# A token tile's latent norms and transposes stand behind the next tile's products, with a second pair of PSUM banks, and the first output row is written ahead of the last head's end

## The chip, the core and the metric

The kernel runs on one core of one Trainium2 chip. The metric is the device time of the whole kernel in microseconds (us). One core has a matrix engine (PE, with its weight loads listed apart as PEld), a vector engine (DVE), a scalar engine (ACT), a general engine (POOL) and DMA queues, of which SP's is the main one. Each engine takes its own instructions strictly in the order in which they stand, and waits on semaphores for the others.

## What is computed

A decoder trunk of two layers on 1024 tokens of width 1024. The second layer's mixer is a multi-head latent attention, and the change lies in it:

```python
def mla_mixer(h, cos, sin, w_in, q_norm_g, kv_norm_g, w_uq, w_ukv, w_out):
    proj = h @ w_in                                   # 1024 -> 384 + 256 + 64
    c_q, c_kv, k_rope = proj[..., :384], proj[..., 384:640], proj[..., 640:]
    q = (rmsnorm(c_q, q_norm_g) @ w_uq).reshape(B, T, 8, 128 + 64)
    kv = (rmsnorm(c_kv, kv_norm_g) @ w_ukv).reshape(B, T, 8, 128 + 128)
    ...
    q_rope = apply_rope(q_rope, cos[:, :, None, :], sin[:, :, None, :])
    k_rope = apply_rope(k_rope, cos, sin)
    o = causal_mla_attention(q_nope, q_rope, k_nope, k_rope, v)
    return o.reshape(B, T, 8 * 128) @ w_out
```

Around it stand a gated DeltaNet layer, two gated feed-forward blocks and the adaLN modulation, none of which the change touches.

## The kernel before

Every product is made three times over, on operands split in a high and a low part (`mm3`: high with high, high with low, low with high).

**The latent stage** is `mla_in`. The 1024 tokens are eight tiles of 128, taken in the order 0, 2, 4, 6, 1, 3, 5, 7; I call them step 0 to step 7. For a tile, `norm` loads the row, normalizes it, transposes it in eight 128x128 blocks (tile `nrm_p`), applies shift and scale on ACT (`nrm_h`) and splits it (`whi`, `wlo`); `norm` of a tile stands one tile ahead. Then come the **products** of the tile: 24 matmuls with 384 columns into one bank (`pq`, the query latent) and 24 with 320 columns into another (`pk`, the key latent and the key's rope part; both tiles have the name `pq` in the trace). Then come what I call the tile's **latents**, in seven pieces:

1. The query latent is squared and summed on ACT (L211), its 1/rms is made by a small DVE and a small POOL instruction (L213, L219), ACT scales it into the tile `mx` (L1189), and PE transposes it in three blocks ("x3", L1192).
2. The same for the key latent, with two transposes ("x2"). `mx` has one buffer, so that the key's square (which uses `mx` as scratch) waits until PE has read the query's `mx` for x3.
3. DVE multiplies each transposed latent by its gain (`mhx`), and both are split into `cq` and `ckv`.
4. The key's rope part is turned by DVE (L1112 to L1114), copied by ACT (L1115), and transposed by PE ("krt", one block, L1200).
5. Nine matmuls make the rope part of the query for all heads from `cq` ("wqr", 512 columns, tile `pr`).
6. DVE turns it (six instructions), ACT copies it (`rt`, L1115), and PE transposes it in eight blocks ("rt", L1211).
7. ACT and DVE split that into `qr`, and SP stores it.

Six PSUM tiles of a tile's latents come from the pool `pd`, which has four banks; `pq` has two, and `nrm_p` two. After the eight tiles, `mla_kq` makes head 0's keys and queries in two halves of 512 tokens (the first needs tiles 0 to 3, which are the steps 0, 4, 1 and 5, the second the steps 2, 6, 3 and 7), and `mla_v` the values of the first two heads (both into `nrm_p`).

**The attention** (`mla_attn`) goes through eight heads with four query blocks each; scores, softmax and the product with the values of different blocks are kept apart by a list `late`. Behind the last head stands the output projection, eight rows of 128 tokens (`out_row`: it loads the heads' outputs and the residual row, splits, multiplies with the first four heads' weights into two `pd` banks and adds).

What stands in the source is not quite what the engines get: the framework places instructions by priority and readiness in a time of its own, and may put a later piece of source ahead of an earlier one that isn't ready. The order that comes out is fixed when the program is built.

Of the kernel before, what the change touches and what calls it, by code (L numbers as in the profile page):

```python
# [9 lines left out]
F32 = mybir.dt.float32  # L10
# [9 lines left out]
P = 128  # L20
T = 1024
D = 1024
NT = T // P
KT = D // P
# [5 lines left out]
QR, KVR, RP = 384, 256, 64  # L30


class Trunk:
# [1099 lines left out]
    def mla_in(self):  # L1133

        nc, tc, a, v = self.nc, self.tc, self.a, self.nc.vector
        self.hq = [self.mla_st.enter_context(tc.tile_pool(name="hq", bufs=1))]
        self.hv = [self.mla_st.enter_context(tc.tile_pool(name="hv", bufs=1))]
        mp = self.mp = self.mla_st.enter_context(tc.tile_pool(name="mp", bufs=1))
        self.cq = [mp.tile([P, 3, T], F32R, name=f"cq{i}") for i in range(2)]
        self.ckv = [mp.tile([P, 2, T], F32R, name=f"ckv{i}") for i in range(2)]  # L1140
        self.kr = [mp.tile([P, T], F32R, name=f"kr{i}") for i in range(2)]
        self.qr_dram = self.dram.tile([P, H, T], F32, name="qr_dram")
        gqs = self.const.tile([P, 3], F32, name="gqs")
        v.tensor_scalar(out=gqs, in0=self.gq, scalar1=float((128 + 64) ** -0.5), op0=ALU.mult, scalar2=None)
        with ExitStack() as st:
            pool = st.enter_context(tc.tile_pool(name="mn", bufs=2))
            ps = st.enter_context(tc.tile_pool(name="mnp", bufs=2, space=PSUM))
            shift = self.mod[1, 0]
            A = self.norm_coef(self.gmix[1], self.mod[1, 1], "Am1")
            w = self.mw  # L1150
            src = a["mla_w_uq"][0].rearrange("(r p) (h n) -> p r h n", p=P, n=192)[:, :, :, 128:192]
            wqr = [self.load_w(src[:, r], shape=(H, 64), pool=pool, bufs=1, tag=f"wqr{r}_") for r in range(3)]

            def norm(t):
                x = self.mwp.tile([P, D], F32, name="xin", bufs=1)
                nc.sync.dma_start(out=x, in_=self.x_dram[t])
                y = self.mwp.tile([P, D], F32, name="nrm_x")
                r = self.rstd_of(x, self.mwp, junk=y)
                v.tensor_scalar(out=y, in0=x, scalar1=r, op0=ALU.mult, scalar2=None)
                hi = self.wsp.tile([P, KT, P], F32R, name="whi")  # L1160
                lo = self.wsp.tile([P, KT, P], F32R, name="wlo")
                for k0 in range(0, KT, 4):
                    pt = ps.tile([P, 4, P], F32, name="nrm_p")
                    h = self.mwp.tile([P, 4, P], F32, name="nrm_h")
                    for k in range(4):
                        kt = k0 + k
                        nc.tensor.transpose(pt[:, k], y[:, kt * P:(kt + 1) * P], self.ident)
                    for k in range(4):
                        kt = k0 + k
                        nc.scalar.activation(out=h[:, k], in_=pt[:, k], func=AF.Identity, scale=A[:, kt:kt + 1],  # L1170
                                             bias=shift[:, kt:kt + 1])
                    self.split(h, hi[:, k0:k0 + 4], lo[:, k0:k0 + 4])
                return hi, lo
            order = (0, 2, 4, 6, 1, 3, 5, 7)
            ahead = norm(order[0])
            for i, t in enumerate(order):
                hi, lo = ahead
                if i + 1 < NT:
                    ahead = norm(order[i + 1])
                lt = [(hi[:, kt], lo[:, kt]) for kt in range(KT)]  # L1180
                pq = ps.tile([P, QR], F32, name="pq")
                self.mm3(pq, lt, [(w[kt][0][:, 0:QR], w[kt][1][:, 0:QR]) for kt in range(KT)])
                pk = ps.tile([P, KVR + RP], F32, name="pq")
                self.mm3(pk, lt, [(w[kt][0][:, QR:], w[kt][1][:, QR:]) for kt in range(KT)])
                ts = slice(t * P, (t + 1) * P)
                for src, n, g, dst in ((pq, QR, gqs, self.cq), (pk[:, 0:KVR], KVR, self.gkv, self.ckv)):
                    y = pool.tile([P, n], F32, name="mx", bufs=1)
                    r = self.rstd_of(src, pool, n, junk=y)
                    nc.scalar.activation(out=y, in_=src, func=AF.Copy, scale=r)  # L1189
                    pt = self.pd.tile([P, n // P, P], F32, name="pd")  # L1190
                    for j in range(n // P):
                        nc.tensor.transpose(pt[:, j], y[:, j * P:(j + 1) * P], self.ident)  # L1192
                    h = pool.tile([P, n // P, P], F32, name="mhx", bufs=1)
                    v.tensor_tensor(out=h, in0=pt, in1=g.rearrange("p (a o) -> p a o", o=1).broadcast_to(
                        [P, n // P, P]), op=ALU.mult)
                    self.split(h, dst[0][:, :, ts], dst[1][:, :, ts])
                kr = pool.tile([P, 1, 2, 64], F32, name="krt")
                self.rope(kr, pk[:, KVR:].rearrange("p (a b) -> p a b", a=1), t, pool, 1)
                pt = self.pd.tile([P, P], F32, name="pd")
                nc.tensor.transpose(pt, kr.rearrange("p a b c -> p (a b c)"), self.ident)  # L1200
                self.split_ps(pt, self.kr[0][:, ts], self.kr[1][:, ts])

                pr = self.pd.tile([P, H, 64], F32, name="pd")
                self.mm3(pr, [(self.cq[0][:, r, ts], self.cq[1][:, r, ts]) for r in range(3)], wqr)
                rt = pool.tile([P, H, 2, 64], F32, name="rt", bufs=1)
                self.rope(rt, pr, t, pool, H)
                qr = pool.tile([P, H, P], F32R, name="qr", bufs=1)
                for h0 in (0, 4):
                    pt = self.pd.tile([P, 4, P], F32, name="pd")
                    for i in range(4):  # L1210
                        nc.tensor.transpose(pt[:, i], rt[:, h0 + i].rearrange("p b c -> p (b c)"), self.ident)  # L1211
                    qh = qr[:, h0:h0 + 4]
                    nc.scalar.copy(qh, pt)
                    v.tensor_tensor(out=qh[64:128], in0=pt[64:128], in1=qh[64:128].bitcast(F32), op=ALU.subtract)
                nc.sync.dma_start(out=self.qr_dram[:, :, ts], in_=qr.bitcast(F32))

            A, B, C = [self.mwp.tile([P, D], F32, name=n, **kw).bitcast(F32R)
                       for n, kw in (("nrm_x", {}), ("nrm_x", {}), ("xin", {"bufs": 1}))]
            r2, r3, r22 = [lambda y: y.rearrange("p (r n) -> p r n", n=P)] * 2 + [
                lambda y: y.rearrange("p (r h n) -> p r h n", r=2, n=P)]  # L1220
            self.kq, self.V = {}, {}
            for g in (self.mla_kq(0, ps, self.kq, ((r2(A[:, 0:256]), r2(A[:, 256:512])),
                                                        (r3(A[:, 512:896]), r3(B[:, 512:896]))), "nrm_p", 2),
                      self.mla_v(0, ps, self.V, (r22(B[:, 0:512]), r22(C[:, 0:512])), "nrm_p", 2)):
                for _ in g:
                    pass
# [117 lines left out]
    def mla_attn(self, right):  # L1344

        nc, tc, a = self.nc, self.tc, self.a
        with ExitStack() as st:
# [4 lines left out]
            early = ExitStack()  # L1352
# [11 lines left out]
            kq, V, late = self.kq, self.V, []  # L1364
            for h in range(H):
# [13 lines left out]
                    late.append((h, qq, pes, V[h // 2], wk, pb))  # L1379
                for _ in steps:  # L1380
                    pass
            self.mla_pv(*late[0])
            self.mla_pv(*self.mla_pt(*late[1]))
            early.close()

            self.out_pools(1, right)
            w_out = a["mla_w_out"][0]
            gate = self.gate_row(1, 2, self.wraw, "wraw", None)
            ws = self.out_w((0, 1), w_out, gate)
# [5 lines left out]
                self.split(raw, w[:, 0], w[:, 1])  # L1395
                ws.append((w[:, 0], w[:, 1]))
            self.bank = lambda: self.pd.tile([P, 512], F32, name="pd")
            for t in range(NT):
                x = self.mp.tile([P, 3, T], F32R, name=f"cq{t % 2}")[:, 0].bitcast(F32)
                o = self.mp.tile([P, 2, T], F32R, name=f"ckv{t % 2}")[:, :, 0:512].rearrange("p i (h t) -> p i h t", h=4)  # L1400
                self.out_row(t, 0, ws, self.x_dram[t], x, self.wraw.tile([P, 4, P], F32, name="wraw"), o[:, 0], o[:, 1],
                             self.bank)
                nc.sync.dma_start(out=self.x_dram[t], in_=x)
                if t == 2:
                    self.ow = self.out_w((4, 5), w_out, gate, self.own)
            self.ow += self.out_w((6, 7), w_out, gate)
# [101 lines left out]
```

## Time and profile before

| | before |
|---|---|
| device time, median of 3 runs | 2616.04 us (2610.63 to 2622.59) |
| the profiled execution: device time | 2613.28 us |
| its span, first to last instruction | 2611.6 us |
| PE busy | 2505.5 us, 96% of the span |
| DVE busy | 1962.5 us, 75% |
| ACT busy | 1173.5 us, 45% |
| mean granted PE clock | 0.988 of full |

The latent stage lies about from 1461 to 1586 us of the span, and the passage from the attention to the output rows about from 1815 to 1850. A row of a timeline gives the start, the duration, the engine, the line, the operation, the tiles (out<-in) and the count; in brackets behind it stands the idle time of the engine just before, and what ended it. Matmuls overlap: one begins before the one ahead of it ends, so the distance of two starts, not the duration, is what a matmul costs in a run of them.

### The profile page before, as it was taken

How to read it: one execution, taken by the hardware profiler on the slowest of the kernel's cores; microseconds unless marked ns; L12 is line 12 of the kernel's file. 1: busy time of each engine (PE TensorE's matmuls, PEld its weight loads, DVE VectorE, ACT ScalarE, POOL GpSimd, SP SyncE). 2: the span in 40 equal slices, each digit the busy share in tenths (PEclk: the TensorE clock that was granted, in tenths of full speed). 3: DMA queues.
4: the chain of work that ended last, by engine and by line, in shares of the span. 5: the costliest groups of instructions: out<-in, count | busy, mean ns of one | idle time of the engine just before them, and what ended most of it. 6: DMA issues, size and time to landing. Idle time of an engine off the chain costs nothing.

```text
span 2611.6 us, 35555 instructions
## 1 busy us (share of the span) xinstructions
PE 2505.5 (96%) x12757; PEld 2058.1 (79%) x12757; DVE 1962.5 (75%) x3748; ACT 1173.5 (45%) x2374; POOL 171.5 (7%) x322
## 2 busy tenths in 40 slices
PE   6999999999999999999999899999999999999998
PEld 5777777777778888888888798888779888887886
DVE  5787789888758888877586766668577777774778
ACT  5555454555465222322344665555283332332343
POOL 1211111221000000000000010000010000000000
PEclk8999999999999999999999999999999999999999
DMA  6111222331454544544945521112643332336634
GB/s 228 41 33 33 75 79 85 89 102 62 153 181 142 182 153 155 160 147 156 314 146 153 155 70 60 47 51 87 216 157 96 108 108 93 108 104 224 226 94 145
DMA packets 258705, 327.62 MB, mean 125 GB/s; under 512 B 17578, under 2 KB 176448, under 8 KB 258528
## 3 DMA queue, kind: packets, MB, share of 16 engines
q1 hardware_dynamic: 235840, 284.37, 34.7%
q10 hardware_dynamic: 22688, 40.97, 4.2%
q8 instruction: 101, 1.65, 0.3%
q14 instruction: 76, 0.62, 0.1%
HBM read 247.16 MB, written 78.14 MB: 125 GB/s over the span
## 4 chain that ended last, share of the span: by engine, by line
PE 77%; DVE 11%; ACT 4%; DMA 3%; issue 2%; POOL 2%; ACTq 0%; POOLq 0%; DVEq 0%; SPq 0%
PE pd L971 14%; PE nrm_p L202 14%; PE pj L202 14%; PE pd L202 10%; PE P L202 8%; PE pd L1288 3%; PE po L202 2%; DVE cacc L334 2%; PE pq L202 1%; PE tp L1331 1%; DVE X L423 1%; DVE st L421 1%; ACT Xs L441 1%; DVE wlo L178 1%; PE d L511 1%
## 5 line engine op out<-in xcount | busy, mean ns | idle before, releaser
L971 PE MATMUL pd<-wlo,gh 128*128 128x512 f32 x616 | 243.9, 396 | 2.5 <-DVE wlo L178 2.0
L971 PE MATMUL pd<-whi,gl 128*128 128x512 f32 x616 | 241.3, 393 | 0.9 <-DVE gl L178 0.9
L971 PE MATMUL pd<-whi,gh 128*128 128x512 f32 x616 | 236.9, 394 | 3.7 <-ACT gh L177 3.3
L202 PE MATMUL pj<-hThi,whi 128*128 128x512 f32 x480 | 197.0, 410 | 0.0
L202 PE MATMUL pj<-hThi,wlo 128*128 128x512 f32 x480 | 196.5, 409 | 0.0
L202 PE MATMUL pj<-hTlo,whi 128*128 128x512 f32 x480 | 196.0, 408 | 0.0
L177 ACT CAST gh<-wraw 128x1024 fp32r<-128x1024 f32 x84 | 82.3, 979 | 247.4 <-PE pd L971 209.2
L177 ACT CAST whi<-wraw 128x1024 fp32r<-128x1024 f32 (+3 forms) x105 | 100.8, 961 | 143.8 <-DMA wraw<-in_ffn_w_gate_dram 54.2
L178 DVE TENSOR_TENSOR gl<-wraw,gh 128x1024 fp32r<-128x1024 f32 x84 | 95.2, 1133 | 63.9 <-ACT gh L177 63.4
L971 PEld LDWEIGHTS pd<-wlo,gh 128*128 128x128 f32 x616 | 116.3, 189 | 33.3 <-DVE wlo L178 8.1
L219 POOL TENSOR_TENSOR nrm_r<-nrm_r,mh 128x1 f32<-128x1 f32 x56 | 37.4, 669 | 1585.3 <-DVE nrm_r L213 965.7
L971 PEld LDWEIGHTS pd<-whi,gh 128*128 128x128 f32 x616 | 116.2, 189 | 30.4 <-ACT gh L177 4.2
L178 DVE TENSOR_TENSOR wlo<-wraw,whi 128x1024 fp32r<-128x1024 f32 (+3 forms) x105 | 117.5, 1119 | 28.6 <-ACT whi L177 26.4
L971 PEld LDWEIGHTS pd<-whi,gl 128*128 128x128 f32 x616 | 116.3, 189 | 26.6 <-DVE gl L178 1.5
L202 PE MATMUL nrm_p<-T,xrow 128*128 128x512 f32 (+1 forms) x576 | 133.7, 387 | 0.0
L202 PE MATMUL nrm_p<-T,ow_hi 128*128 128x512 f32 (+1 forms) x600 | 132.0, 369 | 0.0
L202 PE MATMUL nrm_p<-T,ow_lo 128*128 128x512 f32 (+1 forms) x552 | 125.8, 376 | 0.0
L202 PEld LDWEIGHTS nrm_p<-T,xrow 128*128 128x128 f32 x576 | 105.3, 189 | 23.5
L202 PEld LDWEIGHTS nrm_p<-T,ow_hi 128*128 128x128 f32 x600 | 103.8, 189 | 20.6 <-ACT fh L791 0.2
L202 PEld LDWEIGHTS nrm_p<-T,ow_lo 128*128 128x128 f32 x552 | 98.0, 189 | 20.4
L334 DVE SCALAR_TENSOR_TENSOR cacc<-cr,cwc,cacc 128x512 f32<-128x512 f32 x144 | 108.5, 760 | 3.3 <-ACT cacc L332 2.8
L202 PEld LDWEIGHTS pj<-hTlo,whi 128*128 128x128 f32 x480 | 92.0, 192 | 15.4
(531 smaller groups left out, 6399.0 us busy)
## 6 DMA issues: line engine op xcount, KB each, us to landing
wraw<-in_ada_w_dram SPq DMA_DIRECT2D x80, 512.0 KB, 4.1
wraw<-in_ffn_w_gate_dram SPq DMA_DIRECT2D x44, 512.0 KB, 3.9
wraw<-in_ffn_w_up_dram SPq DMA_DIRECT2D x44, 512.0 KB, 4.4
gd_S<-sx ACTq DMA_DIRECT2D x88, 256.0 KB, 2.5
B<-in_ffn_w_down_dram SPq DMA_DIRECT2D x40, 512.0 KB, 6.8
wraw<-gd_S SPq DMA_DIRECT2D x40, 512.0 KB, 5.1
gd_A<-co ACTq DMA_DIRECT2D x66, 256.0 KB, 2.1
wraw<-in_gdn_w_in_dram SPq DMA_DIRECT2D x32, 512.0 KB, 4.6
```

The source lines that it names most:

```text
L177: nc.scalar.copy(hi, raw)
L178: nc.vector.tensor_tensor(out=lo, in0=raw, in1=hi.bitcast(F32), op=ALU.subtract)
L202: nc.tensor.matmul(out, l, r, start=(i == 0), stop=(i == len(seq) - 1))
L219: self.nc.gpsimd.tensor_tensor(out=out, in0=in_, in1=self.mh[:, 0:in_.shape[1]], op=ALU.pow)
L334: nc.vector.scalar_tensor_tensor(out=acc, in0=cr[:, j:j + 512], scalar=self.cw[:, j, ch:ch + 1], in1=acc, op0=ALU.mult, op1=ALU.add)
L421: v.tensor_tensor(out=t[:, 0:n], in0=Lr[:, j, j + 1:32].rearrange("p (i o) -> p i o", o=1).broadcast_to([P, n, 8]), in1=X[:, j:j + 1].broa ...
L423: v.tensor_tensor(out=X[:, j + 1:32], in0=X[:, j + 1:32], in1=t[:, 0:n], op=ALU.subtract)
L441: nc.scalar.copy(Xs[pb, :, b * 32:b * 32 + 32].rearrange("p m (r c) -> p m r c", c=8), Xn[pb, :, :, mh].rearrange("p c r m -> p m r c"))
L511: nc.tensor.matmul(psn, kd, y, start=True, stop=True)
L971: nc.tensor.matmul(acc[t], x[:, j, ts], y[:, j], start=(j0 + j == 0 and k == 0), stop=(j0 + j == NJ - 1 and k == 2))
L1288: nc.tensor.matmul(sc[:, 0:nm], q[:, ts], k[:, cs], start=(i == 0), stop=(i == 4 and not last))
L1331: nc.tensor.transpose(pt[:, kt - k0], pes[qi][:, kt * P:(kt + 1) * P], self.ident)
```

## The change

In `mla_in` the body behind the products becomes a function `latents(t, pq, pk)`, and the loop calls it one tile late: tile t's latents are written behind the products of the tile after it. So two tiles' products are alive at once. Those of the steps 0, 2, 4, 6 go to the two banks of `pq` as before, those of the steps 1, 3, 5, 7 to two of the four banks of `pd`, which the latents use as well. In `mla_attn` the output weights' preparation and output row 0 move ahead of the last query block's end.

```diff
+            def latents(t, pq, pk):
+
                 ts = slice(t * P, (t + 1) * P)
...
+            order = (0, 2, 4, 6, 1, 3, 5, 7)
+            ahead, last = norm(order[0]), None
+            for i, t in enumerate(order):
+                hi, lo = ahead
+                if i + 1 < NT:
+                    ahead = norm(order[i + 1])
+                lt = [(hi[:, kt], lo[:, kt]) for kt in range(KT)]
+                b, nm = ((ps, "pq"), (self.pd, "pd"))[i % 2]
+                pq = b.tile([P, QR], F32, name=nm)
+                self.mm3(pq, lt, [(w[kt][0][:, 0:QR], w[kt][1][:, 0:QR]) for kt in range(KT)])
+                pk = b.tile([P, KVR + RP], F32, name=nm)
+                self.mm3(pk, lt, [(w[kt][0][:, QR:], w[kt][1][:, QR:]) for kt in range(KT)])
+                if last:
+                    latents(*last)
+                last = t, pq, pk
+            latents(*last)
...
-            self.mla_pv(*late[0])
-            self.mla_pv(*self.mla_pt(*late[1]))
-            early.close()
-
-            self.out_pools(1, right)
...
-            for t in range(NT):
+
+            def row(t):
...
+            self.mla_pv(*late[0])
+            row(0)
+            self.mla_pv(*self.mla_pt(*late[1]))
+            early.close()
+            self.out_pools(1, right)
+            for t in range(1, NT):
+                row(t)
```

The next rows are those of PE, of before, at a tile in the middle of the latent stage: from one tile's rt to the next tile's krt. Matmuls into `pq` are the products of the next tile.

```order
L1211 MATMUL pd<-ident,rt 128x128 x8
L202 MATMUL pq<-wmi_hi,whi 128x320
...
L1192 MATMUL pd<-ident,mx 128x128 x3
L1167 MATMUL nrm_p<-ident,nrm_x 128x128 x8
L202 MATMUL pq<-wmi_hi,whi 128x384
...
L1192 MATMUL pd<-ident,mx 128x128 x2
L202 MATMUL pq<-wmi_hi,whi 128x384
...
L1200 MATMUL pd<-ident,krt 128x128
```

And these are PE's of the change, from step 2's rt through step 3's latents to step 5's products (line numbers moved: x3 and x2 are L1183, krt L1191, rt L1202).

```order
L1202 MATMUL pd<-ident,rt 128x128 x8
L1183 MATMUL pd<-ident,mx 128x128 x3
L1167 MATMUL nrm_p<-ident,nrm_x 128x128 x5
L1183 MATMUL pd<-ident,mx 128x128 x2
L1191 MATMUL pd<-ident,krt 128x128
L202 MATMUL pd<-wqr_hi,cq_13670 128x512
...
L202 MATMUL pq<-wmi_hi,whi 128x384
...
L1202 MATMUL pd<-ident,rt 128x128 x8
L202 MATMUL pd<-wmi_hi,whi 128x384
```

Nine products and eight transposes stood between x3 and x2, now five transposes; fifteen products stood between x2 and krt, now nothing. The products of step 5 (into `pd`) come only behind step 3's last transposes.

At the end of the stage, PE of before, from the last tile's products to its last transposes; matmuls into `nrm_p` are `mla_kq`'s.

```order
L202 MATMUL pq<-wmi_hi,wlo 128x320
L1192 MATMUL pd<-ident,mx 128x128 x3
L202 MATMUL nrm_p<-ckv_13672,nrm_x 128x512
...
L1192 MATMUL pd<-ident,mx 128x128 x2
L202 MATMUL nrm_p<-cq_13670,nrm_x 128x512
...
L1200 MATMUL pd<-ident,krt 128x128
L202 MATMUL pd<-wqr_hi,cq_13670 128x512
...
L202 MATMUL nrm_p<-ckv_13672,nrm_x 128x512
...
L1211 MATMUL pd<-ident,rt 128x128 x8
```

And PE of the change at the same place, from step 7's products through step 6's and into step 7's latents.

```order
L202 MATMUL pd<-wmi_hi,wlo 128x320
L1183 MATMUL pd<-ident,mx 128x128 x5
L1191 MATMUL pd<-ident,krt 128x128
L202 MATMUL pd<-wqr_hi,cq_13670 128x512
...
L1202 MATMUL pd<-ident,rt 128x128 x8
L1183 MATMUL pd<-ident,mx 128x128 x5
L202 MATMUL nrm_p<-ckv_13672,nrm_x 128x512
L202 MATMUL nrm_p<-cq_13670,nrm_x 128x512
L1191 MATMUL pd<-ident,krt 128x128
```

Two tiles' latents now stand behind the last products, step 6's with no other work of PE between its pieces. The whole order of the change on PE, as what stands between a tile's pieces ("384" and "320" are products with so many columns, "norm" 128x128 transposes of a later tile's `norm`, "kq" matmuls of `mla_kq`; the pieces of one tile never stand between another's):

| step | x3 to x2 | x2 to krt | wqr to rt |
|---|---|---|---|
| 0 | 8 norm, 5 of 384 | 11 of 384 | 8 of 384, 12 of 320 |
| 1 | 8 norm | 4 norm | 4 norm, 18 of 384 |
| 2 | 6 of 384, 8 norm | 5 of 320 | 19 of 320, 3 norm |
| 3 | 5 norm | nothing | 18 of 384 |
| 4 | 6 of 384 | 6 of 320 | 18 of 320 |
| 5 | nothing | 2 kq | 13 kq |
| 6 | nothing | nothing | nothing |
| 7 | nothing | 2 kq | 13 kq |

At the end of the attention, PE of before, behind the last but one query block's products (`tp` are transposes of the softmax, `po` the products with the values, matmuls into `pd` the output rows'):

```order
L1331 MATMUL tp<-ident,pe 128x128 x7
L202 MATMUL pd<-whi,ckv_18416 128x512
L202 MATMUL pd<-V_18406,ckv_18416 128x512 x3
...
L1331 MATMUL tp<-ident,pe 128x128 x4
L202 MATMUL pd<-V_18412,ckv_18416 128x512
...
L202 MATMUL po<-PT_18320,V_17042 128x256
L202 MATMUL pd<-V_18412,ckv_18416 128x512
L202 MATMUL pd<-whi,ckv_18452 128x512
```

And the change there:

```order
L202 MATMUL pd<-whi,ckv_18349 128x512
L202 MATMUL pd<-V_18317,ckv_18349 128x512 x3
L202 MATMUL pd<-V_18323,ckv_18349 128x512 x3
L1338 MATMUL tp<-ident,pe 128x128 x7
L202 MATMUL pd<-whi,ckv_18452 128x512
...
L1338 MATMUL tp<-ident,pe 128x128 x8
L202 MATMUL pd<-V_18317,ckv_18452 128x512
L202 MATMUL po<-PT_18384,V_17042 128x256
```

Output rows' matmuls stood among the last head's in both; a few more stand ahead of the last transposes now. On SP's queue one store of the last head's output moves behind three loads, and nothing else changes there.

## Rows read from the trace of the kernel before

**Rows 1.** Windows: from:to, length, busy us of PE PEld DVE ACT POOL, PEclk, DMA.

```profile
1475.20:1575.90 100.70, 96.22 (x590) 88.26 (x591) 66.47 (x199) 68.26 (x178) 11.86 (x22) 1.00 0.24 73
1815.00:1850.00 35.00, 34.19 (x213) 28.99 (x212) 25.99 (x54) 18.01 (x46) 1.55 (x6) 1.00 0.34 110
```

**Rows 2.** Waits of PE, 1475.2 to 1575.9: total us, times, longest.

```profile
PE pd L1192 <- ACT mx L1189: 3.9, 5, 2.5
```

**Rows 3.** Timeline of step 0, all engines, from x3 to x2.

```profile
1477.70 0.55 PE L1192 MATMUL pd<-ident,mx 128*128 128x128 f32 x3 [2.53 <-ACT mx L1189]
...
1478.35 0.38 ACT L211 ACTIVATE mx<-pq 128x256 f32<-128x256 f32 x1
...
1478.85 0.15 DVE L213 TENSOR_SCALAR nrm_r<-nrm_ss 128x1 f32<-128x1 f32 x1
...
1479.09 0.55 POOL L219 TENSOR_TENSOR nrm_r<-nrm_r,mh 128x1 f32<-128x1 f32 x1 [2.05 <-DVE nrm_r L213]
...
1479.67 0.48 ACT L1189 ACTIVATE mx<-pq,nrm_r 128x256 f32<-128x256 f32 x1
...
1480.20 0.44 PE L1192 MATMUL pd<-ident,mx 128*128 128x128 f32 x2
```

**Rows 4.** Timeline of step 6, from x2 to the copy for krt.

```profile
1555.52 0.44 PE L1192 MATMUL pd<-ident,mx 128*128 128x128 f32 x2 [0.43 <-ACT mx L1189]
...
1556.65 0.19 DVE L1114 TENSOR_TENSOR krt<-rp,rp 128x32 f32<-128x32 f32 x1
...
1556.88 0.25 ACT L1115 COPY krt<-krt 128x64 f32<-128x64 f32 x1
```

**Rows 5.** Timeline of step 7, from wqr's last matmul to rt.

```profile
1571.84 0.39 PE L202 MATMUL pd<-wqr_hi,cq 128*128 128x512 f32 x1
...
1572.26 0.42 DVE L1112 TENSOR_TENSOR rp<-pd,cos 128x256 f32<-128x256 f32 x1 [1.47 <-PE pd L202]
...
1574.38 0.62 ACT L1115 COPY rt<-rt 128x512 f32<-128x512 f32 x1 [0.85 <-DVE rt L1114]
...
1575.06 1.09 PE L1211 MATMUL pd<-ident,rt 128*128 128x128 f32 x8
```

**Rows 6.** Timeline, step 0's copy for krt, and x3 and x2 of step 1.

```profile
1482.40 0.26 ACT L1115 COPY krt<-krt 128x64 f32<-128x64 f32 x1
...
1489.21 0.49 PE L1192 MATMUL pd<-ident,mx 128*128 128x128 f32 x3
...
1492.43 0.44 PE L1192 MATMUL pd<-ident,mx 128*128 128x128 f32 x2 [0.30 <-ACT mx L1189]
```

**Rows 7.** Timeline of PE in unbroken runs, for the distance of starts.

```profile
1474.14 1.03 PE L1167 MATMUL nrm_p<-ident,nrm_x 128*128 128x128 f32 x8
...
1479.13 0.34 PE L202 MATMUL pq<-wmi_hi,whi 128*128 128x384 f32 x1
...
1480.00 0.34 PE L202 MATMUL pq<-wmi_hi,wlo 128*128 128x384 f32 x1
...
1485.10 0.31 PE L202 MATMUL pq<-wmi_hi,wlo 128*128 128x320 f32 x1
...
1487.89 0.31 PE L202 MATMUL pq<-wmi_hi,whi 128*128 128x320 f32 x1
...
1572.75 2.22 PE L202 MATMUL nrm_p<-cq,nrm_x 128*128 128x512 f32 x9
```

**Rows 8.** Timeline of PE, one wait in the feed-forward stage.

```profile
1946.83 0.39 PE L202 MATMUL P<-B,wlo 128*128 128x256 f32 x1 [2.79 <-DVE nrm_r L213]
```

**Rows 9.** Windows of 2 us behind that wait, columns as in rows 1.

```profile
1946.00:1948.00 2.00, 1.17 (x9) 1.18 (x10) 2.00 (x5) 1.85 (x4) 1.84 (x2) 0.94 0.57 229
1948.00:1950.00 2.00, 2.00 (x11) 1.90 (x11) 1.90 (x5) 2.00 (x4) 0.00 (x0) 0.50 0.02 6
1950.00:1952.00 2.00, 2.00 (x15) 2.00 (x15) 2.00 (x4) 1.16 (x3) 0.00 (x0) 0.71 0.61 180
```

More of the change, by code (lines that the diff above doesn't have):

```diff
@@ L1173, in norm @@
                 return hi, lo
[L1174 to L1184, printed above, removed]
+            def latents(t, pq, pk):
                 ts = slice(t * P, (t + 1) * P)
```

## The prediction

> **What bounds the kernel now.** I read the page first: PE is busy in 96% of the span, and PE carries most of the chain that ended last. A change gains here what PE idles, and loses what it makes PE wait. So I read the windows of the two stretches that the change touches. In the latent stage, from the end of step 0's products to the first `mla_v` matmul, PE is busy in 96.22 of 100.70 us, so it idles 4.48 us. In the passage to the output rows it idles 0.81 of 35 us [rows 1]. All other work of PE is the same matmuls as before. More than 5.3 us can therefore not be won by filling PE, and that is 0.2% of the time. PE's waits put 3.9 of the 4.48 us on the scaled latent that x3 and x2 transpose [rows 2], and 2.53 of it on one place, step 0's x3 [rows 3].
>
> What a measurement of this kernel can tell from no change I take as 0.5%, 13 us.
>
> **What a tile's latents ask of PE.** Between x3 and x2, x2 and krt, and wqr and rt, a tile's latents leave PE for ACT, DVE and POOL and come back, and something else has to stand on PE there. From the timelines I take two prices for each place: bare, where little else stood on ACT and DVE, and loaded, where the next tile's `norm` stood among them.
>
> (a) x3 to x2: the key's square waits for x3 to leave `mx`, then come the sum, DVE, POOL, the scale. At step 0, x2 starts 2.50 us behind x3's start; less x3's own 0.55, PE needs cover for 1.95 us, bare [rows 3]. At step 1 it starts 3.22 us behind, and PE idled 0.30 us, so that this was a true end of a wait; less 0.49, that is 2.73 us loaded [rows 6].
>
> (b) x2 to krt: at step 6 x2 ended at 1555.96 and ACT's copy at 1557.13, with DVE's six small instructions between: 1.2 us bare [rows 4]. At step 0 x2 ended at 1480.64 and the copy at 1482.66: 2.0 us loaded [rows 3, 6].
>
> (c) wqr to rt: 1572.23 to 1575.06, 2.83 us [rows 5]. ACT did little else there, so I use it as both.
>
> Cover on PE, by the distance of starts [rows 7]: a product with 384 columns 0.174 us (five in 0.87), with 320 columns 0.147 (nineteen in 2.79), eight `norm` transposes 1.03, a `kq` matmul 0.23 (nine in 2.22, the last 0.39 of it). Before, nine products and eight transposes covered (a) with 2.6 us, fifteen products (b) with 2.6, and 21 products (c) with 3.1; hence the few tenths of idle time in the middle of the stage.
>
> **What the change removes.** Step 0's x3 no longer stands ahead of step 1's products: 48 products, 7.7 us, go first, and its 2.53 us go. I give the change the whole 4.48 us.
>
> **What it adds.** The products of the steps 1, 3, 5, 7 need two `pd` banks, from the same pool of four that the latents go through. So in the order that comes out, the products of step 3 stand behind all of step 1's latents, step 5's behind step 3's, step 7's behind step 5's. Products then come in pairs and latents in pairs, and the odd steps' latents find little left to cover them. At the end step 6's and step 7's latents both stand behind the last products, and the first half of `mla_kq`, which covered the last tile before, has been used up at step 5. Cover from the table of the change, against the needs; what is missing in us, bare and loaded:
>
> - step 0: cover 1.90, 1.91, 3.15: 0.05 and 0.9
> - step 1: 1.03, 0.5, 3.6: 1.6 and 3.2
> - step 2: 2.07, 0.74, 3.2: 0.5 and 1.9
> - step 3: 0.65, 0, 3.1: 2.5 and 4.1
> - step 4: 1.04, 0.88, 2.65: 1.4 and 3.0
> - step 5: 0, 0.46, 3.0: 2.7 and 4.3
> - step 6: 0, 0, 0: 6.0 and 7.6
> - step 7: 0, 0.46, 3.0: 2.7 and 4.3
>
> The sums are 17.4 and 29.3 us. At the steps 0 to 4 `norm` of later tiles still stands among ACT's instructions (five scale-and-shift instructions ahead of step 3's key latent), so I take loaded there: 13.1. At the steps 5 to 7 ACT has nothing of `norm` left, so bare: 11.4. Together 24.5 us of new idle time.
>
> **The clock.** A wait of 2.79 us for DVE [rows 8] was followed by windows of 2 us at 0.94, 0.50 and 0.71 of full clock, so near its lower level of 1.2 GHz [rows 9]; less full clock that is 0.12 + 1.00 + 0.58, 1.7 us lost. The wait of 2.53 us at step 0 was followed by none, since the stage's mean is 1.00 [rows 3, 1]. The new waits at the steps 3 and 5 to 7 are 1.2 to 2.9 us, several in a row with little work between. I count one to two such dips, 2 us; the bounds are 0 and 6.
>
> [...]
>
> **The output row.** Output rows' matmuls stood among the last head's before as well; the order was already so. A few more now stand ahead of the last transposes, which can only take from the 0.81 us that PE idled there [rows 1]: I count 0.3 us won, between 0.8 won and 0.3 lost. On SP one store moves behind three loads; the heads that it holds are read only in the second half of the projection, eight rows later, so it waits for nobody. Pools opened later cost nothing.
>
> **Sum.** 24.5 - 4.5 + 2 - 0.3 = 21.7 us. The profiled execution took 2613.28 us, so 2635 us. That execution lies 2.8 us under the median of 2616.04; I set the forecast on the execution.
>
> **Rivals.**
>
> *Bare waits only.* If each handoff takes its bare price, since ACT and DVE, with PE slower, have emptied their queues, and no dip comes: 17.4 - 4.5 - 0.3 = +12.6, 2626 us, within 0.5%. For it speaks that ACT is busy in only 68 of 100.7 us and DVE in 66 [rows 1]. Against it: they take instructions in order, and `norm` of a later tile stands ahead of the piece that PE waits for.
>
> *Everything runs ahead (the other side).* While PE does 7.7 us of another tile's products, ACT and DVE could finish a tile's query and key latents, so that x3 and x2 need no cover; this decides if the key's square can start before PE's x3. Then nothing of (a) and (b) is left, only step 6's (c): 2.8 - 4.5 - 0.3 = -2, 2611 us, not slower. Against it: `mx` has one buffer, so that the key's chain starts behind x3 in each tile, and the rows of step 0 show just that sequence [rows 3].
>
> *Cold clock through the end.* From step 5's x3 to the first `mla_v` matmul stand some 11 us of waits in about 30 us. If PE fell to half its clock over the 19 us of work in there for as much as half of it, that is 9 us more in place of 2, and with loaded prices at the steps 5 to 7 (4.8 more) +33: 2647 us. The Trainium skill has such a case ("TensorE: Matmul & The Clock Gate", "A second HAM failure mode: psum-queue depth-cycling"): small idle times between groups of matmuls that go around the banks make the clock swing. For it here: a fall at 2.79 us [rows 8, 9]. Against it: none at 2.53 us.
>
> **Chances and range.** The forecast (waits about as summed, 2629 to 2642) 0.66; bare waits only 0.15; everything ahead 0.04; cold clock 0.15. Faster by over 0.5% would need 13 us, more than twice what PE idles in both stretches: 0.02, left for what I have not seen. Within 0.5% fall the bare case, the case on the other side but for that, and a small part of the forecast's low end: 0.18. Slower: 0.80. The range runs from 2621, below the bare case by a few us for handoffs that are covered after all, to 2647, the cold case.
>
> **What will show it.** In the profile after: PE's idle time in the latent stage of some 24 us in place of 4.5, ended by ACT at x3/x2 and krt, and by ACT's copy at rt of step 6; the first `mla_v` matmul at about 1597 in place of 1576; the wait of 2.53 us gone; PE clock under 1.00 in a window behind step 5; the passage to the output rows as before. I am wrong if PE idles under 12 us there, or if the second products of a pair stand in time beside the odd steps' latents; and if the stage is as said and the end still isn't, then something downstream gave it back.

## The result and the profile after

The change makes the kernel slower: 2649.64 us, median of 4 runs (2645.94 to 2653.91), against 2619.32 us, median of 4 runs of before (2610.63 to 2623.91). The ratio is 1.011, 95% interval 1.0088 to 1.0132. The forecast was 2635 us, with a range of 2621 to 2647: the direction was right, and the time lies 2.6 us above the range. The profiled execution of the change took 2650.61 us, 37.3 us more than that of before.

Windows of the change, from the end of the `norm` transposes behind step 0's products to the first `mla_v` matmul, and the passage to the output rows (columns as in rows 1):

```profile
1475.20:1610.76 135.56, 110.86 (x593) 97.15 (x591) 68.19 (x200) 69.10 (x178) 13.39 (x22) 0.87 0.18 54
1849.86:1884.86 35.00, 34.20 (x213) 28.98 (x212) 27.30 (x56) 18.46 (x46) 1.55 (x6) 1.00 0.39 128
```

They answer to [rows 1]. The passage is as it was: PE idles 0.80 us of 35, as against 0.81. The latent stage has become 34.9 us longer, and two things are to be read in its row. PE idles 135.56 - 110.86 = 24.70 us in place of 4.48, so 20.2 more. And PE is *busy* 14.6 us longer, with the same matmuls, at a granted clock of 0.87 in place of 1.00.

Waits of PE in that stretch (line waited at, releaser: total us, times, longest), against [rows 2] (L1180 is ACT's scale into `mx`, which was L1189; `rp` is the tile that DVE's turn writes):

```profile
PE pd L1183 <- ACT mx L1180: 14.2, 8, 3.2
PE pd L1191 <- ACT krt L1115: 3.2, 3, 1.5
PE pd L1202 <- ACT rt L1115: 3.0, 2, 2.8
PE nrm_p L202 <- ACT ckv L177: 2.0, 2, 1.0
PE pq L202 <- DVE rp L1112: 1.6, 2, 0.8
PE nrm_p L1167 <- ACT nrm_h L1170: 0.6, 1, 0.6
```

The wait of 2.53 us at step 0's x3 [rows 3] is gone; x2 now waits in all eight tiles.

Timeline of the change at step 3, PE and what it waits for:

```profile
1527.35 0.49 PE L1183 MATMUL pd<-ident,mx 128*128 128x128 f32 x3
1527.67 0.71 PE L1167 MATMUL nrm_p<-ident,nrm_x 128*128 128x128 f32 x5
...
1528.25 0.40 ACT L211 ACTIVATE mx<-pd 128x256 f32<-128x256 f32 x1
...
1528.62 1.86 ACT L1170 ACTIVATE nrm_h<-nrm_p,col,Am 128x128 f32<-128x128 f32 x5
...
1531.09 0.47 ACT L1180 ACTIVATE mx<-pd,nrm_r 128x256 f32<-128x256 f32 x1 [0.20 <-POOL nrm_r L219]
...
1531.61 0.69 PE L1183 MATMUL pd<-ident,mx 128*128 128x128 f32 x2 [3.23 <-ACT mx L1180]
...
1533.82 0.48 PE L1191 MATMUL pd<-ident,krt 128*128 128x128 f32 x1 [1.52 <-ACT krt L1115]
...
1534.52 0.63 PE L202 MATMUL pd<-wqr_lo,cq 128*128 128x512 f32 x1
...
1535.80 0.63 PE L202 MATMUL pd<-wqr_lo,cq 128*128 128x512 f32 x1
```

This is place (a) with the mechanism that was forecast, at more than its loaded price: x2 starts 4.26 us behind x3, and less x3's own 0.49 us that is 3.77 us, against 2.73. The square follows x3 in `mx`, five scale-and-shift instructions of `norm` stand on ACT ahead of the scale, and PE has five transposes to cover it all. Windows of 2 us behind it, columns as in rows 1, against [rows 9]:

```profile
1528.00:1530.00 2.00, 0.38 (x4) 0.14 (x2) 1.94 (x4) 2.00 (x8) 0.00 (x0) 1.00 0.00 1
1530.00:1532.00 2.00, 0.39 (x2) 0.29 (x2) 1.49 (x6) 1.79 (x6) 0.79 (x1) 0.85 0.59 179
1532.00:1534.00 2.00, 0.48 (x4) 0.18 (x2) 1.36 (x7) 1.62 (x6) 0.68 (x1) 0.50 0.72 182
1534.00:1536.00 2.00, 2.00 (x6) 1.61 (x6) 0.83 (x2) 1.25 (x3) 0.14 (x1) 0.50 0.00 0
1536.00:1538.00 2.00, 2.00 (x7) 1.52 (x6) 0.15 (x1) 0.00 (x0) 0.00 (x0) 0.50 0.26 72
1538.00:1540.00 2.00, 2.00 (x13) 2.00 (x12) 1.83 (x6) 0.00 (x0) 0.00 (x0) 0.94 0.20 59
1540.00:1542.00 2.00, 2.00 (x17) 1.97 (x15) 0.26 (x1) 0.80 (x2) 0.00 (x0) 1.00 0.04 8
```

The clock goes to 0.50, its level of 1.2 GHz, and stays there while PE already has work again: in the windows from 1534 to 1538 PE is busy throughout, and its matmuls with 512 columns start 0.43 us apart (three from 1534.52 to 1535.80), where nine of `mla_kq` with as many columns took 0.23 us each at full clock [rows 7]. By such windows through the whole stage there are six dips; each is worth the sum of (1 - clock) x 2 us over its windows. With PE's waits, tile by tile, beside the forecast of the idle time:

| step | PE's waits, us | sum | forecast | dip behind them, us lost |
|---|---|---|---|---|
| 0 | 0.20 | 0.2 | 0.9 | none |
| 1 | 1.07, 0.61, 0.35 | 2.0 | 3.2 | 1500 to 1506: 1.7 |
| 2 | 0.42, 0.81 | 1.2 | 1.9 | none |
| 3 | 3.23, 1.52 | 4.8 | 4.1 | 1530 to 1540: 3.4 |
| 4 | 1.33, 0.81, 0.20 | 2.3 | 3.0 | 1554 to 1560: 1.7 |
| 5 | 3.03, 1.02 | 4.1 | 2.7 | 1564 to 1574: 3.4 |
| 6 | 2.40, 1.29, 2.83 | 6.5 | 6.0 | 1588 to 1594: 1.7, then with step 7 |
| 7 | 2.55, 0.95 | 3.5 | 2.7 | 1596 to 1608, from step 6's rt on: 5.1 |
| sum | | 24.6 | 24.5 | 17.0 |

Of the 17.0 us some fall into the waits themselves; I read the rest as the 14.6 us of longer busy time. So the theory to be tested: the idle time came out as summed, and the miss is the clock, which fell at six places for which I had counted 2 us. The rivals: the longer busy time has another cause than the waits; or part of the loss lies elsewhere than in this stage.

### The profile page after: what moved, and what is told of

Its sections match the earlier page's. It is cut to its first block, busy times and chain, and to the rows that moved or that the text cites. A ratio compares the mean times of both kernels' runs of the same rounds, so it can differ in the third digit from the quotient of the medians.

```text
span 2648.9 us, 35565 instructions
## 1 busy us (share of the span) xinstructions
PE 2522.0 (95%) x12757; PEld 2066.8 (78%) x12757; DVE 1964.1 (74%) x3748; ACT 1173.2 (44%) x2374; POOL 173.0 (7%) x322
## 4 chain that ended last, share of the span: by engine, by line
PE 78%; DVE 11%; ACT 4%; DMA 3%; issue 2%; POOL 2%; POOLq 0%; DVEq 0%; SPq 0%; ACTq 0%
PE pd L971 14%; PE nrm_p L202 14%; PE pj L202 14%; PE pd L202 11%; PE P L202 7%; PE pd L1295 3%; PE po L202 2%; DVE cacc L334 1%; PE tp L1338 1%; DVE st L421 1%; DVE X L423 1%; DVE wlo L178 1%; PE pq L202 1%; ACT Xs L441 1%; POOL nrm_r L219 1%
```

## The experiments

In what follows "the stretch" goes from the last of the `norm` transposes behind step 0's products to the first `mla_v` matmul, 0.2 us more than in [rows 1] for before. It is 100.9 us in the profile of before (from 1475.01) and 135.6 us with the change. Intervals are of 95%.

**Each part alone.** The changed `mla_in` with the old `mla_attn`, and the reverse.

> The first part alone: latents one tile late and odd tiles' products in pd; the end of the attention stands as before. Theory (everything is lost in the latent stage): the whole loss, a ratio to before of 1.009 to 1.013, the first mla_v matmul near 1611 us of the span in place of 1576, PE idle there about 24.5 us and a mean granted clock near 0.87. Rival (a part is lost at the output rows, where the wait at the second half grew from 3.40 to 4.46 us and the end came another 1.4 us later): the ratio comes out at 1.008 or under, the stage unchanged.

> The second part alone: output row 0 and the weights ahead of the last head's end; the latent stage stands as before. Theory: within 0.2% of before (ratio 0.998 to 1.002), the latent stage as before, PE idle in the passage within 0.8 us of before. Rival: the row's loads and the wait at the second half of the output rows cost 3 to 8 us of their own, ratio 1.001 to 1.003 with that wait at 4.4 us or more.

Latents alone: ratio 1.0113 (1.0085 to 1.014), the stretch 135.65 us, PE busy 110.91 of it, clock 0.87, and the same six dips behind the same waits. Row alone: ratio 1.0004 (0.9988 to 1.002), the stretch 100.27 us; PE idles 0.80 us in the passage and 3.37 us at the second half of the output rows, as before (3.40). The whole loss is the latents', and the rival at the output rows falls: the wait at their second half is 4.46 us with the change, but 5.10 us with the latents alone, where the attention is the old one, so that its growth is not the row's.

**Two buffers for `mx`.**

```diff
-                    y = pool.tile([P, n], F32, name="mx", bufs=1)
+                    y = pool.tile([P, n], F32, name="mx", bufs=2)
```

> The change with two buffers for mx, so that the key latent's square and scale need not wait for x3; x3 and x2 then stand together in PE's order and krt comes soon behind them. Theory (the single mx buffer behind x3 makes 14 us of the waits, and these draw most of the clock's fall): the waits at x2 go, those at krt grow by 3 to 5 us, PE idle 12 to 15 us, mean clock 0.93 or over, the first mla_v matmul 12 to 20 us earlier than with the change, ratio 1.003 to 1.007. Rival (the waits come from the missing cover behind the banks and not from mx): the idle time moves to krt and to the products, 20 us or more, clock under 0.90, ratio 1.009 or over.

Ratio 1.0027 (1.0009 to 1.0044), just under what was expected. Window of the stretch and PE's first waits in it:

```profile
1473.38:1584.80 111.42, 100.96 (x593) 90.75 (x591) 65.94 (x199) 66.53 (x177) 11.97 (x22) 0.97 0.22 66
```

```profile
PE pd L202 <- ACT cq L177: 4.0, 4, 1.4
PE pd L1202 <- ACT rt L1115: 3.3, 2, 2.8
PE pd L202 <- ACT mx L1180: 1.5, 1, 1.5
```

The waits at x2 are gone. In all the idle time falls by 14.2 us (24.7 to 10.5), and the busy time by 9.9 (110.9 to 101.0): 24 of the 35 us. One dip is left, behind step 6's rt (2.83 us) and what follows it. The idle time is below the 12 to 15 us that were expected, and the waits did not move to krt, but to `wqr` (4.0 us), one piece later.

**PE kept at work in its waits.** The same waits, filled with matmuls that nobody needs:

```diff
+            def keep(out, n, on):
+                wr = w[0][0]
+                for _ in range(n if on else 0):
+                    nc.tensor.matmul(out, wr[:, 0:P], wr[:, 0:out.shape[1]], start=True, stop=True)
...
+                    keep(pt.rearrange("p a b -> p (a b)"), 16, src is not pq and t in (6, 3, 5, 7))
                     for j in range(n // P):
                         nc.tensor.transpose(pt[:, j], y[:, j * P:(j + 1) * P], self.ident)
```

> The change with PE kept at work in its longest waits: 16 extra matmuls of 256 columns ahead of x2 at the steps 3, 5, 6 and 7, ten of 128 ahead of krt at the steps 3 and 6, eleven of 512 ahead of rt at step 6. They write the PSUM tile that the transposes then overwrite, and add about 11 us of work that nothing needs. Theory (the stage's 14.8 us of longer busy time are the clock's, drawn by the waits): the mean clock rises from 0.87 to 0.95 or over and the first mla_v matmul comes 5 to 12 us earlier than with the change although PE does more, ratio 1.006 to 1.009. Rival (the clock falls for another reason, or the matmuls are longer for another reason than the clock): the clock stays under 0.90, or the first mla_v matmul comes no earlier; ratio 1.011 or over.

Ratio 1.0079 (1.0051 to 1.0106). Window of the stretch, and the same for the extra matmuls alone (PE, PEld, clock, DMA):

```profile
1481.23:1608.04 126.81, 113.71 (x688) 102.16 (x686) 68.43 (x200) 68.37 (x178) 13.29 (x22) 0.99 0.19 58
```

```profile
1481.23:1608.04 126.81, 13.91 (x95) 12.35 (x95) 0.99 0.19 58
```

PE does 95 matmuls more, 13.9 us of them, and is through 8.8 us earlier than with the change. The clock is 0.99, and what is not filler takes 113.71 - 13.91 = 99.8 us in place of 110.9. The extra work stands where PE waited (idle time and filler together are 27.0 us, the waits of the change 24.7), so the dependences are as long as they were and only the clock has changed. This decides between the theory and its rival: the matmuls were longer because the clock fell, and the clock fell because PE waited. It is the trace that shows it; the interval of the ratio overlaps that of the change. The waits of step 1 were not filled, and drew no dip here, so one dip of the five that went is not the filler's. One dip is left, at step 4, whose waits were not filled either:

```profile
1556.07 0.44 PE L1189 MATMUL pd<-ident,mx 128*128 128x128 f32 x2 [1.35 <-ACT mx L1185]
1557.32 0.41 PE L202 MATMUL pq<-wmi_hi,whi 128*128 128x320 f32 x1 [0.81 <-DVE rp L1112]
```

**Half as much filler.** The counts 16, 10 and 11 become 8, 5 and 5.

> As the filled waits, with half as many extra matmuls: 8 ahead of x2 at the steps 3, 5, 6 and 7, five ahead of krt at the steps 3 and 6 and of rt at step 6. It asks what of a wait draws the clock down. If it is the length of one unbroken wait: the waits left are 1.5 us or shorter, the dips at those places go, clock 0.98 or over, the stretch from step 0's products to the first mla_v matmul 126 to 129 us. If it is the share of time that PE idles around a place: the dips stay at half of the places or more, clock 0.90 to 0.95, the stretch 130 us or over.

Ratio 1.0085 (1.0054 to 1.0117). Window of the stretch, and PE's rows at step 7's x2:

```profile
1483.30:1611.09 127.79, 112.15 (x639) 99.22 (x638) 67.54 (x200) 68.46 (x178) 13.22 (x22) 0.95 0.19 58
```

```profile
1598.91 1.22 PE L1177 MATMUL pd<-wmi_hi 128*128 128x256 f32 x8 [0.64 <-DVE qr L1213]
1601.46 0.44 PE L1189 MATMUL pd<-ident,mx 128*128 128x128 f32 x2 [1.33 <-ACT mx L1185]
1602.90 0.64 PE L202 MATMUL nrm_p<-ckv,nrm_x 128*128 128x512 f32 x1 [1.00 <-ACT ckv L177]
```

Four dips of six stay: at the steps 1 and 4, which were not filled, and at 5 and 7, where no wait is longer than 1.33 us, but two or three stand close together; there they are worth 1.7 us each in place of 3.4 and 5.1. The dips of step 3 and of step 6's x2 and krt are gone, and the last begins only at step 7, though a wait of 1.68 us is left at step 6's rt. So neither reading is borne out alone: the length came out as by the first, the clock and the count of dips as by the second. What falls is the first reading in its plain form: these dips follow groups of waits of which none is long. What it is in such a group that draws a dip stays open.

**Only the transposes late.** The squares, scales and the key's turn follow a tile's own products, into SBUF, so that all products go through `pq`:

```diff
-                b, nm = ((ps, "pq"), (self.pd, "pd"))[i % 2]
+                b, nm = ps, "pq"
...
+                now = scaled(t, pq, pk)
                 if last:
                     latents(*last)
-                last = t, pq, pk
+                last = now
```

> The change with the squares, scales and the key's rope turn of a tile written right behind its own products (into SBUF, two buffers each for the two scaled latents), and only the transposes and what follows them one tile late. So the two banks of pq come free early, all products go there, and none goes into pd. Theory (the waits came from the shared pd banks, which made products and latents stand in pairs, and from the chain through the one mx buffer; putting a tile's transposes behind the next products costs nothing by itself): PE idle of 1 to 6 us between step 0's products and the first mla_v matmul, mean clock 0.99 or over, that stretch 97 to 103 us in place of 100.9 before and 135.6 with the change, ratio 0.998 to 1.002. Rival (the delay itself takes the cover away, since x3, x2 and krt of a tile then stand together and wqr waits behind them): PE idle of 10 us or more, clock under 0.98, ratio 1.004 or over.

Ratio 1.0012 (0.9993 to 1.0031). Window of the stretch and the waits:

```profile
1482.72:1589.12 106.40, 101.03 (x593) 91.89 (x592) 65.81 (x198) 67.94 (x175) 11.44 (x22) 0.97 0.23 69
```

```profile
PE pq L202 <- ACT mx L1179: 2.2, 1, 2.2
PE pd L202 <- ACT cq L177: 1.6, 2, 1.4
PE pd L1207 <- ACT rt L1115: 1.2, 1, 1.2
```

PE idles 5.4 us: putting a tile's transposes behind the next products costs no cover by itself, and the rival falls. This edit takes away the single `mx` and the shared banks together, and brings a wait of its own at `pq`. So what the banks cost beyond `mx` isn't told apart; the difference to the run with two buffers is 10.5 to 5.4 us of idle time. The length was missed by 3 us, and the clock too (0.97): two dips, one behind the wait of 2.2 us at step 1's first product, the other at the end of the stretch, behind waits of 1.19, 0.42 and 1.41 us.

**The same with step 1's products in `pd`**, to take that wait away (`b, nm = (self.pd, "pd") if i == 1 else (ps, "pq")`).

> As the early scale, with step 1's products alone in two pd banks, so that they need not wait for step 0's scaled latents to be read out of pq (the wait of 2.16 us there). Theory: that wait and the dip behind it go, PE idle of 2 to 4 us between step 0's products and the first mla_v matmul, that stretch 100 to 104 us (its end keeps the waits of 1.2 and 1.4 us and perhaps a dip), ratio 0.998 to 1.002, so at best level with before. Rival (it beats before): the stretch is under 99 us and the ratio under 0.998.

Ratio 0.9999 (0.9983 to 1.0015): level with before. Window of the stretch, and the longest wait:

```profile
1478.96:1581.99 103.03, 97.73 (x593) 89.07 (x591) 66.00 (x199) 68.31 (x178) 11.45 (x22) 1.00 0.23 72
```

```profile
PE pd L1196 <- ACT mx L1179: 2.1, 1, 2.1
```

The wait moved to step 0's krt, so PE still idles 5.3 us, above the 2 to 4 that were expected, but no dip came, at the end of the stretch neither, where the three waits are 1.19, 0.42 and 1.41 us again. None of these versions beats the kernel before; the 4.5 us that could be won there are below what the runs can tell.

**The kernel before with two buffers for `mx`.**

> The kernel before with two buffers for mx and nothing else changed. Theory (before, products cover the chain through mx but for step 0): the stretch from step 0's products to the first mla_v matmul is 98 to 101 us against 100.9, clock 1.00, ratio 0.998 to 1.002; the wait at step 0's x3 stays near 2.5 us. Rival (mx costs before as well): the stretch is 96.5 us or less, the ratio under 0.998.

Ratio 1.0003 (0.9983 to 1.0022), the stretch 102.28 us, so longer than expected by either. The wait at step 0's x3 is as before, 2.49 us, and windows of 2 us show what came behind it:

```profile
1476.00:1478.00 2.00, 0.37 (x4) 0.37 (x4) 0.40 (x3) 1.00 (x3) 1.06 (x2) 1.00 0.89 296
1478.00:1480.00 2.00, 2.00 (x10) 1.94 (x9) 1.80 (x9) 2.00 (x7) 0.00 (x0) 0.52 0.71 202
1480.00:1482.00 2.00, 2.00 (x9) 1.97 (x8) 1.01 (x3) 0.46 (x2) 0.00 (x0) 0.63 0.00 0
```

In the profile of before the same place, with a wait of 2.53 us [rows 3], shows no dip. The clock is 1.00 in all three windows, of which these are the last two:

```profile
1478.00:1480.00 2.00, 2.00 (x15) 2.00 (x13) 1.35 (x4) 2.00 (x6) 0.55 (x1) 1.00 0.77 218
1480.00:1482.00 2.00, 2.00 (x13) 1.82 (x13) 1.57 (x9) 2.00 (x5) 0.00 (x0) 1.00 0.00 1
```

## Why the prediction was right in direction and short in size

- **What can be won.** Right: 4.5 us, 2.53 of it at one wait, which went.
- **The new idle time.** Right in its places and causes; that the sum agrees to 0.1 us is luck. Between x3 and x2 the chosen prices make 12.8 us, measured 14.2. Between x2 and krt 8.7, measured 7.4 (3.2 at krt, and 4.2 at what stands ahead of it: `norm`, the products that wait for the bank that DVE's turn still reads, and `mla_kq`). At rt 3.0, measured 3.0. Together 24.5 and 24.6. But loaded prices for the steps 0 to 4 were too high in sum (forecast 13.1, measured 10.5; at step 3's x2 too low, 2.08 and 3.23), bare ones for 5 to 7 too low (11.4 and 14.1), and the two errors cancel. ACT had nothing of `norm` left at the steps 5 to 7, as I wrote, but DVE had the tile before: with x3 right behind that tile's rt, DVE does its `qr`, and the gain of the query latent, ahead of the small instruction (L213) of the key's 1/rms. What that one needs, ACT's sum, is ready at 1563.96, and it starts 1 us later. Timeline of the change at step 5, ACT and DVE:

```profile
1563.14 1.30 DVE L1205 TENSOR_TENSOR qr<-pd,qr 64x512 fp32r<-64x512 f32 x2 [0.61 <-ACT qr L1204]
...
1563.75 0.21 ACT L211 ACTIVATION_READ_ACCUMULATOR mx<-pd 128x1 f32 x1
1564.47 0.56 DVE L1185 TENSOR_TENSOR mhx<-pd,gqs 128x384 f32<-128x384 f32 x1
1564.95 0.14 DVE L213 TENSOR_SCALAR nrm_r<-nrm_ss 128x1 f32<-128x1 f32 x1
```

- **The clock: the step that failed.** "I count one to two such dips, 2 us; the bounds are 0 and 6." Measured: six dips, 14.6 us of longer busy time. The price of one dip, 1.7 us [rows 9], was right for three of them; the count was wrong, and so were the lengths: the other three, in which more waits follow inside the dip, cost 3.4 or 5.1 us. I had set the two waits of 2.79 us (a dip) and 2.53 us (none) beside each other as if one wait's length decided, and so counted only the longest new waits. The steps 1 and 4 dip behind waits of 1.07 and 1.33 us with others close by. The filled waits show that PE's waiting is the cause of the dips; that groups of short waits are enough is read from the steps 1 and 4, and from 5 and 7 with half the filler.
- **What the Trainium skill says of such waits.** "TensorE: Matmul & The Clock Gate", section "Loop structure matters more than you think", states of a loop whose next matmuls follow at once that VectorE's copy out of PSUM does not break PE's warmth, and shows PE going cold behind a long DMA wait. It doesn't cover this case: the next matmuls did not follow at once, and all six dips follow waits for ACT or DVE. The case that I named beside the rival of the cold clock, the Trainium skill's "A second HAM failure mode: psum-queue depth-cycling" on the same page, was the nearer one. Here the idle times are handoffs to ACT and not a queue of banks; with two buffers for `mx` most of them go, though the products stay in the same banks.
- **The rival of the cold clock** (2647 us, 0.15) came nearest. From step 5's x3 on the dips cost 3.4 + 1.7 + 5.1 = 10.2 us, against its 9; the further 6.8 at the steps 1, 3 and 4 it had not either. Its nearness is in part luck: it made up for them with 4.8 us of further idle time, of which the total shows nothing.
- **The order's cause.** That `mx` has one buffer was the heart of the argument against "everything runs ahead", and holds: a second buffer takes back 24 of 35 us.
- **The output row.** Right within its bounds: 0.0 in place of the 0.3 won.
- **The base.** The forecast was set on one execution, of 2613.28 us, and is measured against a median of 2619.32. Of the 14.6 us by which the result lies above 2635, 6.0 come from that and 8.6 from the sum (21.7 forecast, 30.3 between the medians). That execution had few dips behind the stretch: by windows of 2 us up to 2600 us they lost 3.4 us there, and 8.5 us each with the change, with the row alone and in the kernel before with two buffers for `mx`.
- **What stays open.** The stretch is 34.7 us longer, the medians differ by 30.3 (by the interval 23 to 35), the profiled executions by 37.3. The start of the stretch, ahead of which nothing is changed, lies between 1473.4 and 1483.3 us in these profiles, so that a few microseconds of such a difference can't be placed. Nor was it settled what makes the same wait draw a dip in one execution and none in another. And the waits stand among transposes, while the filler is other matmuls: no run tells whether the transposes have a part in the dips.

## What to carry to other kernels

Where work is moved so that PE has to wait for other engines, sum the idle time by place, and then price the clock by groups of waits, not by the longest one: here the groups of six of the eight tiles drew six dips, of 1.7 to 5.1 us each, which came to 0.7 us (14.6 / 20.2) for each microsecond of new idle time in this stage. Before a stage is delayed, look for the scratch tile with one buffer that chains its pieces; here a second buffer gave back 24 of 35 us, and scaling early, with two buffers and without the shared banks, 29. And what can be won by filling PE is bounded by its idle time in that stretch, here 4.5 us, which is less than the runs can tell.

## What the runs showed of the hardware that was not expected

The cost of a dip comes in steps: from 1400 to 2600 us of the ten profiles, each lost about 1.7, 3.4 or 5.1 us, and none an amount between. The same wait does not always draw a dip. At step 0's x3, 2.53 us drew none and 2.49 us one of 1.7 us; a wait of 2.16 us drew one and one of 2.11 us none. The three waits at the end of the stretch (1.19, 0.42 and 1.41 us) drew one with the early scale, and none in the next run. The waits of step 1 (1.07, 0.61 and about 0.35 us) drew a dip with the change and with the latents alone, at the same place, and none with the filled waits. And useless matmuls in a wait can shorten a stage: 13.9 us of them, put where PE idled, brought the stretch from 135.6 to 126.8 us.
